# Shifting the weight tiles by 64 bytes within each partition, and lengthening block 0's activation rows to 544 columns

## The chip, the cores and the metric

One core of a Trainium2 chip runs the whole program in one launch. The metric is the device time in microseconds (us), the median of several runs; one more execution was taken with the profiler. TensorE does the matrix multiplies (the profile calls its matmuls PE and its weight loads PEld), VectorE is DVE, ScalarE is ACT, GpSimd is POOL, and SyncE (SP) issues most of the transfers. The local memory has 128 partitions; a tile takes the same byte range in each of them, and "position" below means the byte offset of a tile, or of a row of it, within the partition.

## The reference

One layer of a decoder over a prompt of 2048 tokens with 16 meta tokens ahead of it, and over 8 single sample tokens, all in float32, model width 1024:

```
hn = rms_norm(h);  z = hn @ w_in                       # 1024 x 2560
u, q, f, i, g = split(z)                               # five parts of 512 columns
y5 = GLU(GELU(diagonal complex state space(u)))        # 32 groups of 16 channels
yh = gated linear recurrence(q, f, i) * silu(g)        # 4 heads of 128, chunks of 64
h  = h + concat(y5, yh) @ w_out                        # 1024 x 1024
a, v = split(rms_norm(h) @ w_up)                       # 1024 x 5632
h  = h + (silu(causal conv of width 3(a)) * v) @ w_down   # 2816 x 1024
y  = rms_norm(h)
```

The outputs are y for prompt and samples, and the new states of the state space, the recurrence and the convolution.

## The kernel before

The prompt goes in four blocks of 512 tokens. Block 0 carries 24 more columns (16 meta tokens, 8 samples), so its rows have W = 536 columns; blocks 1 to 3 have 512. In the FFN block 0 keeps 522 of them.

Every product of an activation with a weight is made of three matmuls in a half-split form: weight and activation are each split into a high part and a remainder (`wh`, `wl` for weights; `ah`, `al`, and `gh`, `gl` behind the convolution, for activations), all of type fp32r, and the pairs high-high, high-low and low-high are summed (`PASS`). A matmul has a stationary operand, which a weight load puts into the array, and a moving operand, which streams past it. While one matmul streams, the load for the next one runs.

- `w_unit` (with `split_w`) brings 512 KB of a weight into a staging tile `st` by an SP transfer; ACT writes the high part (line 449) and DVE the remainder (line 83). The tiles `st` (2 buffers), `wh` and `wl` (3 each) are 1024 columns, 4096 bytes, and come from the pool `wp`.
- `fm_mm` (line 480): the weight is stationary, the activation moves, 512 columns in blocks 1 to 3. In block 0 a row is cut: 256 and 280 columns in the input projection, 256 and 266 in the FFN. For each of 8 (in the GLU 4) rows `k` it does the three matmuls.
- `tm_mm` (line 500), in the heads: the activation is stationary (128 tokens), the weight moves, 256 columns.
- `tm_wide` (line 518), the output projection: the activation is stationary, the weight moves, 512 columns.
- the FFN's down projection (line 1233): `gh`, `gl` are stationary, the weight moves, 512 columns.

`new_act` makes `ah` and `al` from the pool `actp` (2 buffers each); a tile is always 8·PW columns, and its eight rows `k` lie 536 columns (2144 bytes) apart for block 0 and 512 columns (2048 bytes) apart otherwise. Pools are laid out one behind the other in the order in which they are opened: `cst`, `wp`, `actp`, then all others. In the program before, `wp` begins at byte 21888 (171·128) and `actp` at byte 54656 (427·128); all sizes in `wp` and `actp` are multiples of 128 bytes. So every `wh` and `wl`, every row of `ah` and `al` in blocks 1 to 3, and every `gh` and `gl` begins at 0 modulo 128. Taken modulo 256 these beginnings are all 128. In block 0 the rows k = 0 to 7 begin at 0, 96, 64, 32, 0, 96, 64, 32 modulo 128.

The work runs in this order: the norm, four heads and the state-space input of a block, with the state space of the block before it woven between (0 to some 1040 us; the output projection of block 0 stands at 477 to 530 us); then the FFN in two passes, blocks 0 and 1 first (`ffn(0)`), blocks 2 and 3 second. Each FFN pass runs over six parts of 3 or 4 column groups of 128: up projections (line 480), then the down projection (line 1233). The instruction order on each engine is the order of the program text.

Of the kernel before, what the change touches and what calls it, by code (L numbers as in the profile page):

```python
# [9 lines left out]
F32 = mybir.dt.float32  # L10
# [10 lines left out]
META = 16  # L21
NS = 8
W = META + BT + NS
PW = W
MT, SP = BT, BT + META
FM_, FS = BT, BT + 2
FF = 2816
# [10 lines left out]
def kernel(  # L38
# [7 lines left out]
    nc = tc.nc  # L46
    pool = lambda name, bufs, **kw: ctx.enter_context(tc.tile_pool(name=name, bufs=bufs, **kw))
    cst = pool("cst", 1)
    wp = pool("wp", 2)
    actp = pool("actp", 2)  # L50
    x4p = pool("x4p", 2)
    nt = pool("nt", 4)
# [57 lines left out]
    def v3(t, a, b):  # L110
        return t[:, :a * b].rearrange("p (a b) -> p a b", a=a)
# [168 lines left out]
    def s5_setup():  # L280
# [18 lines left out]

        both = actp.tile([128, 8 * PW], F32, name="both", tag="ah")  # L300
        wall, dall = both[:, :2048], both[:, 2048:4096]
# [36 lines left out]

        kt_ = actp.tile([128, 8 * PW], F32, name="kt_", tag="al")
        kv_ = kt_[:16, :2048].rearrange("c (g m) -> c g m", g=32)  # L340
# [124 lines left out]
    def new_act(b):  # L465

        pw = PW if b == 0 else BT
        return tuple(v3(actp.tile([128, 8 * PW], F32R, name=n), 8, pw) for n in ("ah", "al"))

# [638 lines left out]
    pool = lambda name, bufs: ctx.enter_context(tc.tile_pool(name=name, bufs=bufs))  # L1108
# [200 lines left out]
```

## Time and profile before

| | |
|---|---|
| time, median of 3 runs | 2577.67 us (2573.76 to 2584.75) |
| the profiled execution: its own time | 2582.91 us |
| its span, first to last instruction | 2581.2 us |
| mean granted TensorE clock | 0.983 |
| PE busy | 2463.4 us, 95% of the span |
| DVE busy | 1450.7 us, 56% |
| ACT busy | 902.9 us, 35% |

Matmuls overlap in the pipeline, so a matmul's listed duration is longer than the distance from its start to the start of the next. The pace below is always that distance: the length of an unbroken stretch divided by its number of matmuls.

### The profile page before, as it was taken

What the parts mean: (1) busy time and instruction counts of PE and PEld (TensorE: products, weight loads), DVE (VectorE), ACT (ScalarE), POOL (GpSimd) and SP (SyncE); (2) the same over time, 40 slices, a digit from 0 to 9 for tenths busy, and PEclk for the clock granted to TensorE, in tenths of its full rate; (3) what the DMA queues carried; (4) which work ended last, traced back from release to release, by engine and by line L of the source; (5) the groups of instructions that cost most, each with busy time, mean ns of one, the idle gap of its engine ahead of it and who ended that gap; (6) DMA issues with size and microseconds to landing.
All of it is one profiled execution on the core that took longest, in us unless ns stands there. A gap on an engine that the chain in (4) does not pass through costs nothing.

```text
span 2581.2 us, 33858 instructions
## 1 busy us (share of the span) xinstructions
PE 2463.4 (95%) x13515; PEld 2099.6 (81%) x13515; DVE 1450.7 (56%) x2950; ACT 902.9 (35%) x1550; POOL 168.9 (7%) x252
## 2 busy tenths in 40 slices
PE   7896998999998989899999999999999999999998
PEld 6785876788887878788989888889888888888886
DVE  6875588678679678464333433344943334333344
ACT  3544354444435435242313222223531313131222
POOL 1232100100000001100000000000310000000000
PEclk9997999999999999999999999999999999999999
DMA  4346433644564562631111111111531111111112
GB/s 122 101 133 184 106 118 125 167 144 128 135 224 133 144 222 87 237 116 59 50 42 50 50 41 44 51 37 50 175 121 49 50 47 46 47 49 49 41 53 78
DMA packets 251260, 252.13 MB, mean 98 GB/s; under 512 B 11303, under 2 KB 208751, under 8 KB 246998
## 3 DMA queue, kind: packets, MB, share of 16 engines
q1 hardware_dynamic: 241088, 220.42, 28.3%
q0 software_dynamic: 9840, 29.48, 3.5%
q8 instruction: 106, 1.74, 0.3%
q14 instruction: 52, 0.43, 0.1%
q10 hardware_dynamic: 174, 0.06, 0.0%
HBM read 216.41 MB, written 33.27 MB: 97 GB/s over the span
## 4 chain that ended last, share of the span: by engine, by line
PE 69%; DVE 12%; issue 5%; ACT 4%; DMA 3%; POOL 1%; SPq 0%; POOLq 0%; ACTq 0%; DVEq 0%
PE mm L480 41%; PE mm L1233 9%; PE hg L1233 9%; PE hg L518 2%; PE mm L518 2%; PE mm L500 1%; DVE hf L655 1%; DVE sB L86 1%; DVE wl L83 1%; DVE sA L908 1%; POOL rstd L544 1%; DVE sA L86 1%; DMA h_d<-x 1%; PE mm L537 1%; PE tp L570 1%
## 5 line engine op out<-in xcount | busy, mean ns | idle before, releaser
L480 PE MATMUL mm<-ah,wh 128*128 128x512 f32 (+3 forms) x2320 | 818.2, 353 | 6.3 <-ACT ah L575 4.2
L480 PE MATMUL mm<-ah,wl 128*128 128x512 f32 (+3 forms) x2320 | 815.0, 351 | 1.5 <-DVE wl L83 1.5
L480 PE MATMUL mm<-al,wh 128*128 128x512 f32 (+3 forms) x2320 | 814.5, 351 | 0.8 <-DVE al L83 0.7
L449 ACT ACTIVATE wh<-st 128x1024 fp32r<-128x1024 f32 (+1 forms) x264 | 276.1, 1047 | 727.3 <-PE mm L480 313.0
L83 DVE TENSOR_TENSOR wl<-st,wh 128x1024 fp32r<-128x1024 f32 (+1 forms) x264 | 318.3, 1206 | 369.3 <-ACT wh L449 366.9
L480 PEld LDWEIGHTS mm<-ah,wh 128*128 128x128 f32 x2320 | 441.4, 190 | 61.7 <-ACT ah L575 4.8
L480 PEld LDWEIGHTS mm<-ah,wl 128*128 128x128 f32 x2320 | 440.9, 190 | 57.0 <-DVE wl L83 2.2
L480 PEld LDWEIGHTS mm<-al,wh 128*128 128x128 f32 x2320 | 441.1, 190 | 55.0 <-DVE al L83 1.4
L86 DVE TENSOR_TENSOR c<-c,mm 128x512 f32<-128x512 f32 (+1 forms) x110 | 63.5, 579 | 211.5 <-PE mm L480 210.1
L500 PE MATMUL mm<-wh,ah 128*128 128x256 f32 x512 | 147.7, 289 | 3.6 <-ACT hg L694 3.2
L500 PE MATMUL mm<-wl,ah 128*128 128x256 f32 x512 | 146.6, 287 | 1.8 <-DVE wl L83 1.8
L500 PE MATMUL mm<-wh,al 128*128 128x256 f32 x512 | 146.4, 286 | 0.0
L1233 PE MATMUL mm<-wh,gh 128*128 128x512 f32 x352 | 137.4, 390 | 0.0
L1233 PE MATMUL hg<-wh,gl 128*128 128x512 f32 x352 | 137.1, 390 | 0.0
L1233 PE MATMUL hg<-wl,gh 128*128 128x512 f32 x352 | 137.1, 390 | 0.0
L1233 PE MATMUL mm<-wl,gh 128*128 128x512 f32 x352 | 137.1, 389 | 0.0
L1233 PE MATMUL mm<-wh,gl 128*128 128x512 f32 x352 | 137.1, 389 | 0.0
L1233 PE MATMUL hg<-wh,gh 128*128 128x512 f32 x352 | 137.0, 389 | 0.0
L80 DVE TENSOR_TENSOR hacc<-hacc,hg 128x512 f32<-128x512 f32 x96 | 65.8, 685 | 88.3 <-PE hg L1233 87.8
L1171 ACT ACTIVATE c<-c 128x512 f32<-128x512 f32 x88 | 55.6, 632 | 144.5 <-DVE c L1170 144.5
L500 PEld LDWEIGHTS mm<-wh,ah 128*128 128x128 f32 x512 | 99.0, 193 | 5.4 <-ACT hg L694 3.4
L80 DVE TENSOR_TENSOR hacc<-hacc,mm 128x512 f32<-128x512 f32 x96 | 65.6, 684 | 66.1 <-PE mm L1233 65.9
(397 smaller groups left out, 3571.0 us busy)
## 6 DMA issues: line engine op xcount, KB each, us to landing
st<-in_ffn_w_up_dram SPq DMA_DIRECT2D x96, 512.0 KB, 3.9
big<-tab_d SPq DMA_DIRECT2D x32, 1156.0 KB, 5.1
st<-in_w_in_dram SPq DMA_DIRECT2D x48, 512.0 KB, 5.6
st<-in_ffn_w_down_dram SPq DMA_DIRECT2D x40, 512.0 KB, 3.5
st<-in_w_in_dram SPq DMA_DIRECT2D x64, 256.0 KB, 3.2
st<-in_w_out_dram SPq DMA_DIRECT2D x32, 512.0 KB, 3.9
x<-in_x_prompt_dram SPq DMA_DIRECT2D x30, 512.0 KB, 4.6
h_d<-x POOLq DMA_DIRECT2D x16, 512.0 KB, 4.7
```

What stands on the lines that cost most here:

```text
L80: tt_(o, a, b, op=OP.add)
L83: tt_(o, a, b, op=OP.subtract)
L86: tt_(o, a, b, op=OP.mult)
L449: ACT(hi[:, :n], st[:, :n], AF.Copy)
L480: mm(p[:, :n], w[wi][:, k, :], a[ai][:, k, c0:c0 + n], start=(i == 0), stop=(i == 3 * nk - 1))
L500: o = mm(dst, lhs(ai, k), (hi, lo)[wi][:, kk, :], start=(i == 0), stop=(i == tot - 1))
L518: mm(pb[t], lhs(ai, k, t), wu[wi][:, kk, :], start=(k == 0 and j == 0), stop=(k == 7 and j == 2))
L537: mm(dst[:m], stat[:, k, :m], w[:, kk, :], start=(i == 0), stop=(i == tot - 1))
L544: nc.gpsimd.tensor_tensor(r, r, mhalf[:ss.shape[0], :n], op=OP.pow)
L570: nc.tensor.transpose(p[:, k, :], x[:, kk * 128:kk * 128 + 128], ident)
L1171: ACT(c, c, AF.Silu)
L1233: mm(ps_[t], gs[b, f0 + k][ai][:, t * 128:t * 128 + 128], wus[i][wi][:, kk, :], start=(k == 0 and j == 0), stop=(k == nf - 1 and j == 2))
```

## The change

Two tiles of 64 bytes that nothing writes or reads are put into pools of their own, one ahead of `wp` and one ahead of `actp`. `wp` moves by 64 bytes, to 64 modulo 128; `actp` moves by 128, and stays at 0 modulo 128. PW grows from 536 to 544, so the rows of block 0 lie 2176 bytes (17·128) apart, all at 0 modulo 128; each of the four buffers grows by 256 bytes, so the pools behind `actp` move by 1152 bytes (9·128) in all. Modulo 256 `wh` and `wl` then begin at 192, `ah`, `al`, `gh` and `gl` at 0; in block 0 the odd rows `k` at 128.

```diff
-PW = W
+PW = W + 8
...
     cst = pool("cst", 1)
+
+    pads = [pool("pad0", 1).tile([128, 16], F32, name="pad0")]
     wp = pool("wp", 2)
+    pads.append(pool("pad1", 1).tile([128, 16], F32, name="pad1"))
     actp = pool("actp", 2)
```

No instruction and no transfer is added or removed.

## Rows read from the trace of the kernel before

**Rows 1.** The page: span, and busy time (share) and instructions of engines.
```profile
span 2581.2 us, 33858 instructions
...
PE 2463.4 (95%) x13515; PEld 2099.6 (81%) x13515; DVE 1450.7 (56%) x2950; ACT 902.9 (35%) x1550; POOL 168.9 (7%) x252
```
**Rows 2.** The page: the chain that ended last, by engine and by line.
```profile
PE 69%; DVE 12%; issue 5%; ACT 4%; DMA 3%; POOL 1%; SPq 0%; POOLq 0%; ACTq 0%; DVEq 0%
PE mm L480 41%; PE mm L1233 9%; PE hg L1233 9%; PE hg L518 2%; PE mm L518 2%; PE mm L500 1%; DVE hf L655 1%; DVE sB L86 1%; DVE wl L83 1%; DVE sA L908 1%; POOL rstd L544 1%; DVE sA L86 1%; DMA h_d<-x 1%; PE mm L537 1%; PE tp L570 1%
```
**Rows 3.** Busy time by stretch: us, PE, PEld, DVE, ACT, POOL, PEclk, DMA.
```profile
512.00:1040.00 528.00, 499.81 (x2934) 425.89 (x2933) 410.65 (x791) 235.96 (x410) 35.20 (x49) 1.00 0.51 155
...
1100.00:1830.00 730.00, 728.61 (x4162) 637.40 (x4163) 318.89 (x597) 209.24 (x309) 5.93 (x12) 1.00 0.18 56
1830.00:2570.00 740.00, 740.00 (x3275) 612.04 (x3274) 319.03 (x492) 207.15 (x288) 31.04 (x49) 1.00 0.20 63
```
**Rows 4.** Groups by line and shape: count, busy us, mean ns, idle before.
```profile
L480 PE MATMUL mm<-ah,wh 128*128 128x512 f32 x1392 | 549.2, 395 | 0.3 <-ACT wh L449 0.2
...
L500 PE MATMUL mm<-wh,ah 128*128 128x256 f32 x512 | 147.7, 289 | 3.6 <-ACT hg L694 3.2 <-DVE hP L86 0.4
...
L1233 PE MATMUL mm<-wh,gh 128*128 128x512 f32 x352 | 137.4, 390 | 0.0
...
L480 PE MATMUL mm<-ah,wh 128*128 128x256 f32 x464 | 133.7, 288 | 2.0 <-ACT ah L575 2.0
...
L480 PE MATMUL mm<-ah,wh 128*128 128x266 f32 x368 | 105.4, 287 | 0.9 <-DVE c L86 0.9
L518 PE MATMUL mm<-wh,ah 128*128 128x512 f32 x128 | 51.6, 403 | 6.3 <-ACT wh L449 6.3
```
**Rows 5.** The chain in order of time, second FFN pass: start, us, what.
```profile
1939.79 2.72 PE mm L1233 x12
...
1983.31 87.04 PE mm L480 x384
```
**Rows 6.** The chain, first FFN pass: one part's up projections, blocks 0 and 1.
```profile
1225.86 90.19 PE mm L480 x576
```
**Rows 7.** The chain, a head of block 1: line 500.
```profile
277.34 11.51 PE mm L500 x96
```
**Rows 8.** The chain, output projection of block 0 (ends at 530 us).
```profile
498.56 1.39 PE mm L518 x6
499.95 1.40 PE hg L518 x6
```
**Rows 9.** The chain, output projection of block 1 (ends at 730 us).
```profile
711.57 1.36 PE mm L518 x6
712.93 1.36 PE hg L518 x6
```
**Rows 10.** Instructions in order of time, block 0's up projection: start us, us, what.
```profile
1500.60 0.28 PE L480 MATMUL mm<-ah,wh 128*128 128x256 f32 x1
...
1502.02 0.28 PE L480 MATMUL mm<-ah,wh 128*128 128x256 f32 x1
...
1502.38 0.28 PE L480 MATMUL mm<-ah,wh 128*128 128x256 f32 x1
...
1502.74 0.28 PE L480 MATMUL mm<-ah,wh 128*128 128x256 f32 x1
...
1503.08 0.28 PE L480 MATMUL mm<-ah,wh 128*128 128x256 f32 x1
...
1503.43 0.28 PE L480 MATMUL mm<-ah,wh 128*128 128x266 f32 x1
...
1506.41 0.39 PE L480 MATMUL mm<-ah,wh 128*128 128x512 f32 x1
```
**Rows 11.** Instructions in order of time, block 2's heads, behind a stall at 642.08.
```profile
642.39 0.39 PE L480 MATMUL mm<-al,wh 128*128 128x512 f32 x1
...
643.09 0.39 PE L480 MATMUL mm<-al,wh 128*128 128x512 f32 x1
643.31 0.39 PE L480 MATMUL mm<-ah,wl 128*128 128x512 f32 x1
...
644.47 0.39 PE L480 MATMUL mm<-al,wh 128*128 128x512 f32 x1
...
645.38 0.39 PE L480 MATMUL mm<-ah,wl 128*128 128x512 f32 x1
```

## The prediction

> **What bounds the kernel now.** I read the page's busy times first: PE is busy for 95% of the span, DVE for 56% [rows 1]. The chain that ended last says the same by time: PE 69%, DVE 12%, and within it line 480 with 41% and line 1233 with 18% [rows 2]. The stretches tell where this holds. In the two FFN passes, 1100 to 2570 us, PE has no idle time worth naming (728.6 of 730, 740 of 740 us) at a granted clock of 1.00; between 512 and 1040 us it is busy for 499.8 of 528 us, and DVE has 410.7 [rows 3]. So in the FFN every nanosecond per matmul is on the path, and ahead of it perhaps half.
>
> The change touches only where operands stand, so what I need is the pace of the matmuls, start to start, and whether position has a part in it. The chain in order of time gives it without gaps. In the second FFN pass 384 matmuls of 512 columns take 87.04 us, 226.7 ns each, and 12 of the down projection 2.72 us, again 226.7 [rows 5]. The 256-column matmuls of a head take 11.51 us for 96, 119.9 ns each [rows 7]. In all of these, both operands stand at 0 modulo 128.
>
> Block 0 is where the trace shows other positions, and there the pace differs for the same shapes. Its output projection has its stationary rows at 0, 96, 64 and 32 modulo 128 and takes 1.39 or 1.40 us for six, some 232 ns each [rows 8]; block 1, all at 0, takes 1.36 for six, 226.7 [rows 9]. Block 0's up projection goes the other way: 24 matmuls of 256 columns between 1500.60 and 1503.43, 117.9 ns each, against 119.9. Inside that run the row k = 4 (0 modulo 128, 1502.02 to 1502.38) needs 0.36 us for its three, 120 each, and k = 6 (64 modulo 128, 1502.74 to 1503.08) needs 0.34, 113 each [rows 10]. So position does matter, by some 7 ns either way, and the sign hangs on the length.
>
> The Trainium skill, "TensorE: Matmul & The Clock Gate", section "Step-by-step: what each phase is for", says that PE has two independent read ports, so that loading the next weights takes nothing from the running matmul. By it the positions of the two operands would have nothing to do with each other, and the change would be worth 0 us. The trace speaks against it with 113 against 120 ns for one shape [rows 10].
>
> **The change part by part.**
>
> *The pads and the 8 columns.* They add no instruction and no transfer; nothing writes the new bytes. DVE and ACT write and read the moved tiles with the same shapes; the trace has no such operation at 64 modulo 128 against one at 0, so I bound that by the slack: in the FFN DVE is busy for 318.9 of 730 us [rows 3], and even a tenth more would be hidden behind PE. 0 us.
>
> *512-column matmuls.* There are 3·1392 at line 480, 6·352 at line 1233 and 6·128 at line 518 [rows 4]. After the change weight and activation stand 64 apart modulo 128 in all of them. No row shows 512 columns at a constant distance of 64. The bounds: from below, what 64 gave at 256 columns, 120 − 113 = 6.7 ns less, so 220 ns; from above, one such step more, 233.3; the mixed positions of block 0's projection stand at 232 [rows 8].
>
> Two things in the rows make me take the upper end. First, the undisturbed paces are steps of 6.67 ns: 226.7 is 34 of them, 120 is 18, 113.3 is 17. At distance 0 both counts are even, at 64 the one that I have is odd; 512 columns at 64 would then be 33 or 35, 220.0 or 233.3. Second, the shortest distances of start to start in proportion to the columns: the fast 256-column row is 113 [rows 10], and behind a stall, where the 512-column matmuls first run at 231 ns (nine from 642.39 to 644.47) until they fall back into 227, the shortest of them is 0.22 us [rows 11]; in the trace's nanoseconds it is 224, twice 112, and no two 512-column matmuls that follow on each other in the trace stand closer, at whatever position. 220 would be below that. So 33 steps look out of reach, and 35 are left. The nearest row, 232 ns, says the same; I take its 5.5 ns above 226.7 as the price, since some pairs may find no steady pace.
>
> In the FFN that is 22·2·24·3 = 3168 matmuls in the up projections of blocks 1 to 3 and 2112 at line 1233: 5280 · 5.5 ns = +29.0 us, all on the path. Ahead of the FFN 1008 at line 480 and 576 at line 518 are left (block 0's 192 run at 232 already): 1584 · 5.5 ns = 8.7 us, half of it on the path: +4.4 us.
>
> *256-column matmuls.* In block 0's up projections 1056 run at 117.9. Even rows k get weight and activation at the distance that k = 6 has now (64 modulo 256; 113), odd rows 192 modulo 256, which k = 2 has now: bounded by 113 and 120; I take 115 for the mean: 1056 · 2.9 = −3.1 us, with the ends −5.2 and +2.2. Line 500 has 3·512 matmuls [rows 4] at 119.9; the ends are 113 (−10.6 us) and 120 (0); I take half, −5 us, of which half is on the path: −2.5 us. Block 0's own projections ahead of the FFN, 336 more of 256 columns, give −1 us.
>
> *266 and 280 columns.* Block 0's 266-column matmuls take 2.98 us for 24, 124.2 each [rows 10]; their length is no multiple of 64 bytes, so no constant position of theirs is kept from one to the next. Between −7 and +7 ns on 1056, ±7.4 us; I take 0.
>
> One part of the first pass shows the mixture: 90.19 us for 576 [rows 6] is 192 · 117.9 + 192 · 124.2 + 192 · 227.6. I expect 22.1 + 23.8 + 44.6 = 90.5 there.
>
> The sum: 29.0 + 4.4 − 3.1 − 2.5 − 1 = +26.8 us. The profiled execution, 2582.9 us, would become 2609.7; it lies 5.2 us above the median of the runs shown, 2577.67, and from that I forecast 2604 us, 1.0% slower.
>
> **The rivals.**
>
> *A: one step less at 512 columns as well (33, 220 ns).* For it: distance 64 is a clean gain at 256 columns [rows 10], and a cost that arises while the next load runs should not depend on how long the matmul goes on afterwards. Against it: nothing below 224 ns so far [rows 11], and block 0's projection, which has rows at 64 among others, is slower [rows 8]. It gives 5280 · −6.7 = −35.2 us, ahead of the FFN −5, and the 256-column gains, −7: −47 us, 2530 us. It decides wherever a constant 64 makes line 480's stretches of 384 fall below 87.04 us.
>
> The skill's "TensorE: Matmul & The Clock Gate", section "Back-to-back issue gap", gives N/2.4 + 2.5 ns, 215.8 at 512 columns; by that estimate 11 ns per matmul would still be to gain, and A would be worth some −75 us. Rows 5 stand at 226.7 without any idle time.
>
> *B: the 512-column pace holds at 226.7, as an undisturbed stream finds its pace at any constant position, and only the 256-column matmuls gain.* For it: after a stall the pace comes back to 227 by itself (644.47 to 645.38, four in 0.91 us) [rows 11]. Then −6.6 us by the terms above, up to −14: 2571 us.
>
> *C: position relative to the weights is nothing; block 0's odd row distance alone makes the differences.* Then only block 0 changes: 192 matmuls of its output projection gain 5.5 ns, −1 us, its 256-column ones go to 120, +2 us: 2579 us.
>
> **How the numbers follow.** A measurement of this kernel can tell about 0.5%, 13 us, from no change. My forecast, slower by one step or nearly so: 0.55. B: 0.13 and C: 0.09, both within 13 us. A: 0.23, faster. So slower 0.55, same 0.22, faster 0.23. The forecast's own range: from 3 ns on the 5280 (+16, less 4 for the gains at 256) to the full step everywhere with no gain at 256 columns, 5280 · 6.7 + 1584 · 6.7 = +46: 2590 to 2624. Since A alone holds more than 0.2, the range has to reach it: 2528 to 2624.
>
> **What would show it.** In the chain of the second pass the stretches of 384 would read 89.2 to 89.6 us; 84.5 would be A, 87.0 B or C. The stretch of 96 at line 500 would fall from 11.51 towards 10.9; at 11.5 the 256-column term is wrong. Block 0's output projection stays near 1.39 for six, if the distance and not the change of distance is what costs; at 1.36 it is C. Weight loads, DVE and ACT groups should keep their means; DVE's split of the weights growing by over a tenth would show a cost of the new position that I set to 0. The prediction is wrong if the paces of both lengths move the same way.

## The result: 1.2% slower

The changed kernel takes 2610.18 us (median of four runs, 2608.7 to 2613.8) against 2578.11 (2573.76 to 2584.75). The ratio, which like those below is taken from all the runs and not from the two medians, is 1.0119, with a 95% interval of 1.0098 to 1.0140. The forecast was 2604 us. The profiled executions are 2608.7 us after and 2582.9 before, so the profile explains 25.8 us, where the sum had +26.8. The medians differ by 32 us: the profiled execution of before lies 4.8 us above its median, that of after 1.5 us below.

The page of the changed kernel, the rows that answer to [rows 1, 2]: span, busy time by engine, and the chain that ended last by engine.

```profile
span 2607.0 us, 33858 instructions
...
PE 2488.7 (95%) x13515; PEld 2096.6 (80%) x13515; DVE 1451.4 (56%) x2950; ACT 902.7 (35%) x1550; POOL 167.0 (6%) x252
...
PE 71%; DVE 11%; issue 5%; ACT 3%; DMA 3%; POOL 1%; SPq 0%; POOLq 0%; ACTq 0%; DVEq 0%
```

The counts are the same. PE is busy 25.3 us longer, almost the whole 25.8 us of the span; every other engine's busy time moves by 3 us or less. (Lines are 3 further down: 480 is now 483, 500 is 503, 518 is 521, 1233 is 1236.)

The groups of the changed kernel by line and shape (count, busy us, mean ns of one, idle before), beside [rows 4]:

```profile
L483 PE MATMUL mm<-ah,wh 128*128 128x512 f32 x1392 | 557.1, 400 | 0.3 <-ACT wh L452 0.2
...
L503 PE MATMUL mm<-wh,ah 128*128 128x256 f32 x512 | 145.3, 284 | 3.9 <-ACT hg L697 3.4 <-DVE hP L89 0.4
...
L1236 PE MATMUL mm<-wh,gh 128*128 128x512 f32 x352 | 139.2, 395 | 0.0
...
L483 PE MATMUL mm<-ah,wh 128*128 128x256 f32 x464 | 133.8, 288 | 2.1 <-ACT ah L578 2.1
...
L483 PE MATMUL mm<-ah,wh 128*128 128x266 f32 x368 | 106.5, 289 | 0.9 <-DVE c L89 0.9
L521 PE MATMUL mm<-wh,ah 128*128 128x512 f32 x128 | 52.4, 410 | 6.2 <-ACT wh L452 6.2
```

A matmul of 512 columns lasts 5 to 7 ns longer, one of 256 columns at line 503 lasts 5 ns less. The durations overlap, so the cost on the path is in the starts, and the chain shows those without gaps. The chain of the changed kernel in order of time (start, us, what): a head of block 1, the start of the FFN, a part of the first pass, and the second pass. These answer to [rows 5 to 7]. The granted clock of the FFN is 1.00, as it was before.

```profile
275.15 11.30 PE mm L503 x96
...
1107.53 70.09 PE mm L483 x401
1177.62 2.80 PE mm L1236 x12
...
1226.10 91.11 PE mm L483 x576
...
1862.32 87.92 PE mm L483 x384
...
1995.03 89.59 PE mm L483 x384
...
2129.43 87.91 PE mm L483 x384
...
2262.14 89.59 PE mm L483 x384
```

Line 1236 needs 2.80 us for 12, 233.3 ns each (226.7 before). The stretches of 384 need 89.59 (233.3 ns each) or 87.92 (229.0), in turn, where all were 87.04 to 87.09. The part of 576 needs 91.11 against 90.19. The FFN's first unbroken piece starts at 1107.53 us. In the kernel before it starts at 1109.64:

```profile
1109.64 68.95 PE mm L480 x401
```

So in these two executions the part ahead of the FFN is 2.1 us shorter, and all of the loss, 27.9 us, lies in the FFN. From this start to the end of the span it is 1471.6 us before and 1499.5 after. That stretch repeats: in three kernels below that leave the FFN's 512-column distances at 0 it is 1471.6 to 1471.8. The part ahead of it does not: in the first of these three, the rows alone, it ends at 1106.20, 3.4 us earlier than before, with the paces of before in the chain. The 2.1 us are therefore within what executions differ by.

Mean distances from start to start, taken from the instructions in order of time, split it up. Distances longer than about 240 ns at 512 columns and 150 at 256 or 266, at which PE waited, are left out of the means; the counts are of all matmuls.

| matmuls | count | ns before | ns after | us |
|---|---|---|---|---|
| line 1236, 512 columns | 2112 | 226.9 | 233.3 | +13.6 |
| line 483, 512, first pass | 1056 | 227.5 | 233.3 | +6.1 |
| line 483, 512, second pass | 2112 | 226.7 | 231.1 | +9.4 |
| line 483, 256, FFN block 0 | 1056 | 118.0 | 117.6 | −0.4 |
| line 483, 266, FFN block 0 | 1056 | 124.1 | 123.7 | −0.4 |
| line 483, 512, ahead of the FFN | 1008 | 228.6 | 229.4 | +0.8 |
| line 521, 512 | 768 | 228.9 | 233.0 | +3.1 |
| line 503, 256 | 1536 | 119.3 | 114.9 | −6.8 |

The first five rows add up to +28.3 us, within half a microsecond of what the chain says of the FFN.

### The profile page after: what moved, and what is told of

It reads as the page before. It is cut to its first block, busy times and chain, and to the rows that moved or that the text cites. A ratio compares the mean times of both kernels' runs of the same rounds, so it can differ in the third digit from the quotient of the medians.

```text
span 2607.0 us, 33858 instructions
## 1 busy us (share of the span) xinstructions
PE 2488.7 (95%) x13515; PEld 2096.6 (80%) x13515; DVE 1451.4 (56%) x2950; ACT 902.7 (35%) x1550; POOL 167.0 (6%) x252
## 4 chain that ended last, share of the span: by engine, by line
PE 71%; DVE 11%; issue 5%; ACT 3%; DMA 3%; POOL 1%; SPq 0%; POOLq 0%; ACTq 0%; DVEq 0%
PE mm L483 42%; PE mm L1236 9%; PE hg L1236 9%; PE mm L521 2%; PE hg L521 2%; DVE hf L658 1%; PE mm L503 1%; DVE sB L89 1%; DVE wl L86 1%; DVE sA L911 1%; POOL rstd L547 1%; DMA x<-in_x_prompt_dram 1%; DMA h_d<-x 1%; DVE sA L89 1%; PE mm L540 1%
## 5 line engine op out<-in xcount | busy, mean ns | idle before, releaser
L483 PE MATMUL mm<-ah,wh 128*128 128x512 f32 (+3 forms) x2320 | 827.1, 357 | 5.4 <-ACT ah L578 3.3
L452 ACT ACTIVATE wh<-st 128x1024 fp32r<-128x1024 f32 (+1 forms) x264 | 276.0, 1046 | 744.5 <-PE mm L483 325.6
L86 DVE TENSOR_TENSOR wl<-st,wh 128x1024 fp32r<-128x1024 f32 (+1 forms) x264 | 318.2, 1206 | 374.8 <-ACT wh L452 372.3
```

Of the source, the lines that this page charges most:

```text
L86: tt_(o, a, b, op=OP.subtract)
L452: ACT(hi[:, :n], st[:, :n], AF.Copy)
L483: mm(p[:, :n], w[wi][:, k, :], a[ai][:, k, c0:c0 + n], start=(i == 0), stop=(i == 3 * nk - 1))
```

## The experiments

In the compiled kernels the tiles' places can be read. Before, weights, activations and gh/gl all stand at 128 modulo 256 bytes in the partition. After, the weights stand at 192 and the others at 0. "Distance" below is the first byte of the moving operand minus that of the stationary one, modulo 256. After the change it is 64 at line 483 and 192 at lines 503, 521 and 1236 (the odd activation rows of block 0 stand at 128, so that for them 64 and 192 change places at lines 483, 503 and 521). The first four kernels below ran beside one set of runs of the kernel before (2581.32 us), the other four beside another (2580.68).

**The pace by itself.** Nothing but streams of matmuls of 128 rows, 48 of each kind, with the byte offsets of both operands chosen:

```
def run(name, n, mo, so, m=128, count=48):
    ...
    for i in range(count):
        s = so // 4 + 128 * (i % 3)
        nc.tensor.matmul(p[:m, :n], sta[:, s:s + m], mov[:, mo // 4:mo // 4 + n], ...)
```

> Only streams of matmuls, nothing of the reference is computed: 48 at a time of one length, with the moving operand at one position and the stationary one at another, a new weight load before each (three stationaries in turn at the same position modulo 256). Theory 1 (the distance of the two operands modulo 128 sets the pace): 512 columns run at 226.7 ns start to start at distance 0 and 128, at 233.3 (or a cycle of 229 on average) at 64 and 192; 256 columns at 120 and 113 to 115; both operands at 64 go like both at 0; the second stretch at distance 64, entered from another one, has the same pace as the first. Rival 2 (the position of the stationary operand alone, a weight load that starts off a multiple of 128): both at 64 go like 0 against 64, and the moving operand at 64 with the stationary at 0 goes like 0 against 0. Rival 3 (distance modulo 256): 64 and 192 differ, 0 and 128 differ. Stationaries of 40 columns: if the overlap of the whole load with the stream costs, they are faster than those of 128; if only how the two begin, the same. 480 columns, 30 pieces of 64 bytes: theory 1 with even steps at distance 0 gives 32 steps, 213.3, and 31 or 33 at 64, 206.7 or 220.

The chain of this kernel in order of time (start, us, what). A name gives the columns (w 512, n 256), then the offset of the moving and of the stationary operand; "few" is a stationary operand of 40 columns.

```profile
37.10 10.88 PE w_zero_zero L79 x48
47.98 11.20 PE w_zero_sixtyfour L79 x48
59.18 11.16 PE w_zero_onetwentyeight L79 x48
70.34 11.00 PE w_zero_oneninetytwo L79 x48
...
126.17 10.90 PE w_sixtyfour_sixtyfour L79 x48
137.08 10.99 PE w_sixtyfour_zero L79 x48
148.07 10.91 PE w_thirtytwo_thirtytwo L79 x48
...
192.28 11.20 PE w_few_zero L79 x48
...
214.54 5.75 PE n_zero_zero L79 x48
220.29 5.66 PE n_zero_sixtyfour L79 x48
...
260.12 5.75 PE n_sixtyfour_sixtyfour L79 x48
265.87 5.45 PE n_sixtyfour_zero L79 x48
...
282.68 5.45 PE n_zero_sixtyfour L79 x48
...
293.88 5.64 PE n_few_zero L79 x48
```

Four things follow. The place itself is nothing: 0/0, 64/64 and 32/32 all give 226.7 ns (10.88 to 10.91 over 48) at 512 columns and 120 at 256. The distance is what counts, and 64 or 192 in place of 0 makes the one length slower and the other faster: 233.3 or 229.0 at 512, 117.8 or 113.3 at 256. A distance of 128 is not one of 0: 232.5 against 226.7, so modulo 128 is not enough. (Modulo 256 is: in the kernel before the distances of line 480 are 0 and 256 modulo 512, those of line 1233 all 256, and both run at 226.7.) And the length of the weight load has no one sign: with 40 columns to load the stream at distance 0 is slower at 512 columns, 233.3, and faster at 256, 117.5 against 120.0; at distance 192 and 512 columns it ran at 230.4 on average, against 233.3.

One expectation was missed: a second stretch at the same distance was to have the pace of the first. At 512 columns it had (11.20 us twice). At 256 columns the stream with the moving operand at 0 and the stationary one at 64 took 5.66 us behind the stream at 0/0 and 5.45 behind one at 32/0, 117.8 and 113.4 ns each. And 256 columns at distance 32 ran at 120.0 with the offsets 0/224 and at 116.7 with 32/0; whether the places or the streams ahead made that difference is not shown. At 384 columns distance 0 gave 173.3 and distance 192 176.7 ns; at 480 columns 216.7 and 215.9 (means of the last 24), where the rule of odd and even steps had asked for 213.3 and for 206.7 or 220.

**The rows alone.** The change without its pads, so that only block 0's activation rows are longer:

```
-PW = W
+PW = W + 8
```

> The change without the pads: only block 0's rows are 544 columns apart, all operands at distance 0. Theory 1: no slower than before; block 0's output projection from 1.39 to 1.36 us for six (-1 us), its 256-column matmuls from 118 to 120 (+2 us), all other paces at 226.7 and 119.9: 2579 us, ratio 1.000 to 1.002. Rival 4 (the longer rows or larger buffers themselves cost, through the DVE and ACT work on block 0 or the moved pools): a good part of the 32 us shows here, 2590 us or more.

Measured: 2581.06 against 2581.32 us, ratio 1.0003 (0.9993 to 1.0014). The chain of this kernel: a head, block 0's output projection, a part of the first pass, a stretch of the second.

```profile
275.25 11.51 PE mm L500 x96
...
481.62 1.40 PE hg L518 x6
...
1222.24 90.19 PE mm L480 x576
...
1980.15 87.04 PE mm L480 x384
```

The longer rows cost and bring nothing. The expectation of 1.36 for block 0's output projection was missed: a row is now 544 · 4 = 2176 bytes, 128 modulo 256, so every second row still stands at distance 128, which the first experiment shows to be slow at 512 columns.

**Both moved.** Rows as in the change and one pad ahead of all pools, so that weights and activations move by 64 bytes together (against the changed kernel, the second pad is left out):

```
     pads = [pool("pad0", 1).tile([128, 16], F32, name="pad0")]
     wp = pool("wp", 2)
-    pads.append(pool("pad1", 1).tile([128, 16], F32, name="pad1"))
     actp = pool("actp", 2)
```

> The first pad alone, rows of 544: weights, activations and all that lies behind them move by 64 bytes together, so that both stand at 64 modulo 128 and the distance is 0. Theory 1 (distance): paces of 226.7 and 119.9 as before, 2579 us, the same as with the rows only. Rival 2 (absolute position of the weights, or any operand off a multiple of 128): 233 ns at 512 columns, 2605 to 2612 us.

Measured: 2583.20 us, ratio 1.0006 (0.9995 to 1.0017). Its chain:

```profile
277.60 11.51 PE mm L502 x96
...
1941.33 2.72 PE mm L1235 x12
...
1984.85 87.04 PE mm L482 x384
```

All the paces of the kernel before are back, although every operand stands at a new place. With this the loss belongs to the distance between weights and activations.

**The down projection's input moved too.** The change, and a third pad ahead of gh/gl, which makes line 1236's distance 128 and leaves the others:

```
+    pads.append(pool("pad2", 1).tile([128, 16], F32, name="pad2"))
     gp = pool("gp", 4)
```

> The changed kernel with one pad more ahead of the pool of gh and gl: the down projection's operands are at distance 128 modulo 256, 0 modulo 128, all others as in the changed kernel. Theory 1 modulo 128: the down projection (2112 matmuls) goes back from 233.3 to 226.7 ns, -13.9 us, 2596 us; the up projections, the heads and the output projection keep the changed kernel's paces. Rival 3 (modulo 256): the down projection keeps 233.3 or takes a third pace, no gain of over 5 us. Rival 5 (the lost time is not PE's pace but something that the pads do elsewhere): nothing moves, 2610 us.

Measured: 2603.36 us, ratio 1.0089 (1.0073 to 1.0105). Its chain (the down projection stands at line 1237 here):

```profile
275.30 10.90 PE mm L503 x96
...
1952.00 2.80 PE mm L1237 x12
...
1996.80 87.91 PE mm L483 x384
```

Line 1237 does not come back to 2.72, which it had to if 128 were as good as 0. The 6.8 us that this kernel's median is below the changed one's come from elsewhere: every stretch of 384 now takes 87.91 us, at a distance that was not touched, which with the two stretches of 288 is 4.6 us of the 4.9 by which the profiled FFN is shorter. The same distance of 64 thus has two paces, 229.0 and 233.3. That what runs ahead of the stretch has a part in which it is, is a guess at this point.

**What the pace is entered from.** Streams of 512 columns at distance 64, 96 of each, behind streams of another kind, then a grid in which the stationary operand moves by 16 bytes, and three streams in bf16. (`x_down` is at distance 192, `from_down` at 64, entered from 192.)

```
run("x_down", 512, 0, 64, count=48)
run("from_down", 512, 64, 0, count=96)
...
for i in range(16):
    run("x_zero", 512, 0, 0, count=12)
    run(f"grid_{letters[i]}", 512, 0, 16 * i, count=48)
```

> Only streams of matmuls, nothing of the reference is computed. Theory 6 (after the first streams: the distance moving minus stationary modulo 256 sets the pace, and at 64 and 192 there are two steady paces, chosen by the state in which the stretch is entered): 512 columns at distance 64 run at 229.0 in some of the four entries (from distance 0, from 192, from 128, from 256-column matmuls) and at 233.3 in others, each steady for all of its 96; 256 columns at 192 at 113.3 or 117.8 likewise. Rival 7 (one pace for each distance; the two paces seen in the changed kernel come of what else runs): all four entries at 229.0, all three of the short ones at one pace. The sixteen distances in steps of 16 bytes, each entered from distance 0: by theory 6 the moving operand at 0 against 0 alone gives 226.7, all others 229 to 235. bf16, 512 columns: if the steps belong to 4-byte operands, half the bytes leave 216 to 220 ns at any distance; if they belong to the matmul, 226.7 and 233.

The chain of this kernel: the entries, two of the grid's steps, and bf16.

```profile
37.27 22.00 PE from_zero L79 x96
...
70.46 22.40 PE from_down L79 x96
...
104.06 21.98 PE from_half L79 x96
...
131.70 21.99 PE from_short L79 x96
...
201.57 10.88 PE grid_a L79 x48
...
215.17 10.88 PE grid_b L79 x48
...
431.07 9.66 PE half_sixtyfour L91 x44
```

Entered from a distance of 192, the stream stays at 233.3 ns; from 0, from 128 or from 256 columns it takes 229.0. The kernel before this one fits: with line 1237 at distance 128 ahead of it, line 483 keeps the shorter pace. Of the grid's 16 stationary offsets, 0, 16, 144 and 240 run at 226.7 and the other twelve between 228.9 and 234.2; the expectation that all but 0 are slow was missed there, and a stationary offset of 16 bytes had 233.3 in the first measurement. At 256 columns (distance 192) all three entries gave 117.8, as the rival had it; the 113.4 of the first measurement, behind a stream at distance 32, was not tried again. In bf16 the three distances tried (0, 192 and 128) give 215.8 ns each by the starts, so none of the effect shows there; the chain's pieces of bf16 read longer, since the record of a matmul is missing in each stream.

**The heads alone.** In the kernel before, line 500's weight tiles are read 192 bytes further on, with every other distance left as it was:

```
-    def split_w(st, n):
-        hi = wp.tile([128, 1024], F32R, name="wh", bufs=3)
+    def split_w(st, n, at=0):
+        hi = wp.tile([128, 1088], F32R, name="wh", bufs=3)[:, at:at + 1024]
...
-            hi, lo = split_w(st, 1024)
+            hi, lo = split_w(st, 1024, 48)
```

> The kernel before, with weight tiles 64 columns longer, so that only the heads' 256-column matmuls of line 500 read their weights 192 bytes further on (distance 192 modulo 256); all else stays at distance 0. Theory 6: line 500 from 119.9 to 113.3 to 115 ns, 1536 matmuls, -7 to -10 us of PE time, half of it on the path: 2575 to 2578 us against 2581, ratio 0.997 to 0.999; 512-column paces at 226.7. Rival 8 (the heads are bound by DVE and transfers, PE's gain there is given back as waits): 11.51 falls to 10.9 for 96 but the time stays, ratio 0.9995 to 1.0005.

Measured in five rounds: 2576.94 against 2580.68 us, ratio 0.9989 (0.9980 to 0.9998). Its chain:

```profile
272.35 11.30 PE mm L500 x96
...
1978.58 87.04 PE mm L480 x384
```

The gain at 256 columns can be had without the loss at 512: the FFN takes 1471.6 us, as before. Line 500 fell to 116.5 ns on average (119.3 before), short of the 113.3 to 115 expected. The version is below the changed kernel, and below the kernel before by 0.1%, hardly more than the interval: its upper end, 0.9998, does not exclude the rival's 0.9995.

**The pads alone.** The change with rows of 536 columns:

```
-PW = W + 8
+PW = W
```

> The change without the longer rows: the two pads, block 0's rows 536 columns apart as before. By distance: the same paces at 512 columns as in the changed kernel in blocks 1 to 3, block 0 mixed as before: 2606 to 2611 us, ratio 1.010 to 1.012. Rival 4 (the rows of 544 have a good part in the loss): 2600 us or less.

Measured: 2602.43 us, ratio 1.0087 (1.0072 to 1.0102). Its chain:

```profile
1357.24 90.62 PE mm L483 x576
...
1984.69 89.59 PE mm L483 x384
```

The ratio lies below what was expected, 1.010 to 1.012. Part of it is the first pass, with 90.62 for a part of 576 where the change has 91.11: its 512-column matmuls, which stand as in the change but run between other rows of block 0, have 229.3 ns on average and not 233.3. Its FFN takes 1496.3 us against 1499.5. With the rows alone at nothing, the pads carry most of the loss.

**A distance of 128.** The change with pads of 128 bytes in place of 64 and rows of 536 columns, so that outside block 0 all operands stand at 0 modulo 128 as before:

```
-PW = W + 8
+PW = W
...
-    pads = [pool("pad0", 1).tile([128, 16], F32, name="pad0")]
+    pads = [pool("pad0", 1).tile([128, 32], F32, name="pad0")]
...
-    pads.append(pool("pad1", 1).tile([128, 16], F32, name="pad1"))
+    pads.append(pool("pad1", 1).tile([128, 32], F32, name="pad1"))
```

> Pads of 128 bytes in place of 64, rows of 536: weights at 0 modulo 256, activations at 128, all at 0 modulo 128. Theory 1 modulo 128, as predicted with: no change, 2579 us. Modulo 256, by the stream at distance 128 (232.5 ns at 512 columns, 118.6 at 256): 5280 times 5.8 ns in the FFN, +31 us, some +4 ahead of it, -1 at line 500: 2612 us, ratio 1.011 to 1.014, stretches of 384 at 89.3 us.

Measured: 2607.36 us, ratio 1.0107 (1.0094 to 1.0121). Its chain:

```profile
1991.46 89.22 PE mm L483 x384
...
2125.47 89.60 PE mm L483 x384
```

In the whole kernel, too, 128 is as bad as 64: the FFN takes 1500.4 us against 1499.5 of the change. The ratio is just below the 1.011 expected modulo 256 and far from the "no change" expected modulo 128. The prediction's "modulo 128" is wrong.

## Why the prediction was right, and where it was not

*The mechanism.* Right: the paces of both lengths depend on where weights and activations stand to each other, and in opposite directions. Moving both leaves 1.0006, moving them apart with the rows left alone gives 1.0087 (by 64) and 1.0107 (by 128), and a bare stream shows the same 226.7 and 233.3. Its coordinate was wrong. All operands of before stand at one place modulo 256, so its rows could not tell 0 from 128; at line 480 rows k = 4 of block 0 stand 128 from the weights and were taken for rows at 0 [rows 10].

The Trainium skill, "TensorE: Matmul & The Clock Gate", section "Step-by-step: what each phase is for", says that PE reads its two operands through independent ports. What the prediction drew from it, that the operands' places then have nothing to do with each other, does not hold in the bare streams: 226.7 at distance 0 against 233.3 at 192, with nothing else running.

*The step count.* 35 steps of 6.67 ns at 512 columns was right for lines 1236 and 521, for line 483 in the first pass and for half of its stretches in the second; the other half, at 87.92 us, missed the 89.2 to 89.6 that was named as the sign. The rule it came from, odd counts at distance 64, does not hold: 229.0 ns is 34.35 steps, and 480 columns broke it too. The forecast rested on it for the choice between 33 and 35, and the other support, no pair nearer than 224 ns, was the sounder one [rows 11].

*512 columns in the FFN.* Predicted 5280 · 5.5 ns = +29.0 us; measured 13.6 + 6.1 + 9.4 = +29.1. That is partly an accident, since 5.5 ns was the price of block 0's mixed distances: line 1236 lost 6.4 ns, line 483 5.8 in the first pass and 4.4 in the second, where half of the stretches run at 229.0.

*256 columns in block 0's up projections.* Predicted −3.1 us, measured −0.4: the mean is 117.6 ns and not 115. The even rows were to have 113, taken from k = 6. But 256 columns, too, have a longer pace in the bare streams, 117.8, beside 113.3, and the mean lies at the longer one.

*266 columns.* 0 predicted, −0.4 us measured. The part of 576 came to 91.11 and not 90.5; both the 512-column and the 256-column share of it were above their terms.

*Ahead of the FFN.* Predicted +4.4 − 2.5 − 1 = +0.9 us, measured −2.1 in one execution of each, less than the executions differ by. That the sum of 26.8 us came so near to the 25.8 of the profile is luck to that extent. Line 483 lost 0.8 ns there on average and not 5.5; an unbroken stretch of 126 in the chain went from 28.58 to 28.86 us, 226.8 to 229.0 ns each, the shorter of its paces. Line 521 lost 4.1. Line 503 gained 4.4 ns on 1536, 6.8 us against the 5 assumed. How much of each lay on the path was put at half and not measured by itself; the version with the heads alone gained 0.1%, some 3 to 4 us (0.5 to 5 by its interval), with no other term in it.

*Block 0's output projection* stayed at 1.38 to 1.40 for six, as predicted. The reason given was only half of it: with the distance of the change (192 and 64 in turn) it is slow, and with the rows alone (0 and 128 in turn) as well.

*The rivals.* A (220 ns at 512) fell: no stream of 512 fp32r columns ran below 226.7. B (512 finds its pace at any constant distance) fell with the bare streams, which are constant for 48 matmuls and stay at 233.3. C (block 0's rows alone) fell with the rows alone, 1.0003.

*Nothing for the writers.* ACT's and DVE's groups of the changed kernel, the two halves of the weights' split (count, busy us and mean ns of one, idle before):

```profile
L452 ACT ACTIVATE wh<-st 128x1024 fp32r<-128x1024 f32 (+1 forms) x264 | 276.0, 1046 | 744.5 <-PE mm L483 325.6
...
L86 DVE TENSOR_TENSOR wl<-st,wh 128x1024 fp32r<-128x1024 f32 (+1 forms) x264 | 318.2, 1206 | 374.8 <-ACT wh L452 372.3
```

1046 and 1206 ns were 1047 and 1206 before. The new place costs the two engines that write it nothing.

*What stays open.* In the bare streams, one try for each entry, which of its two paces a stream takes goes with the stream ahead of it, but not by a rule that covers the changed kernel: there each stretch of 384 follows line 1236 at distance 192, and they still alternate between 87.92 and 89.59. At line 503 the same 96 matmuls took 11.30 us in the changed kernel and 10.90 with gh/gl moved. That is no effect of the move: up to the FFN's first down projection the two kernels give PE the same instructions at the same places, and in both some stretches of line 503 run at 113.3 and others at 117.8, not the same ones in each. So which pace a stretch takes can differ from one execution to the next. Why the count of steps depends on the distance was not found.

## What to carry to other kernels

A kernel that PE bounds with fp32r operands should have the first bytes of the moving and the stationary operand at the same place modulo 256 wherever it runs 512 columns, and a row length that keeps them there. A padding or another pool order that breaks this costs up to 3% of such a stretch with no other trace than the pace. It can be foreseen from two things: the chain in order of time, divided by its count, and the operands' places in the compiled kernel. Where the kernel before has all its distances at one value, a small stream with nothing else in it prices the new ones.

## What the runs showed of the hardware that was not expected

The pace of a bare stream at 512 fp32r columns lies between 226.7 and 234.2 ns by the distance of its operands alone, at 256 columns between 113.3 and 120.0, and no distance beat equal places at the one or was slower than equal places at the other. (Three other stationary offsets did as well at 512, and one as badly at 256.) One stream has two steady paces at the same places, 229.0 and 233.3 at 512 columns, kept over 384 matmuls, and 117.8 and 113.3 at 256. A stationary operand of 40 columns in place of 128 made the stream at distance 0 slower at 512 columns, 233.3 against 226.7, and faster at 256, 117.5 against 120.0. The bf16 stream stays at 215.8 at each of the three distances tried; that is also what the Trainium skill, "TensorE: Matmul & The Clock Gate", section "Back-to-back issue gap", gives as the warm gap at 512 columns (N/2.4 + 2.5 ns, for a single matmul, without naming the type), and what no fp32r stream here came to.
